# Softmax cross-entropy on one core: loads on two DMA rings, three buffers, a tapered last group and one activation table set

## The chip, the cores and the metric

The kernel runs on one core of a Trainium2 chip. The metric is device time in microseconds (us), lower is better. The times of before agree within 0.03% (2439.7 to 2440.5 us). In the profile, ACT is ScalarE, DVE is VectorE, POOL is GpSimd, SP is SyncE; "ACTq" and "SPq" are the instruction sequencers of ScalarE and SyncE; the timelines list their DMA issues there. A "ring" below is a DMA queue of the page. In these traces the loads that SyncE issues are on q1 (21,168 packets, 1048.65 MB in the kernel before), those that ScalarE issues on q10, and GpSimd's gathers on q0, which the page calls software_dynamic (2048 packets before).

## The reference

For 8192 rows of 32,000 float32 logits, the loss is log(sum(exp(row))) minus the logit at the row's label. The reference subtracts the row's maximum first; both kernels leave that out, and results are correct on the drawn data.

```python
logits_max = np.max(logits, axis=-1, keepdims=True)
log_sum_exp = np.log(np.sum(np.exp(logits - logits_max), axis=-1)) + logits_max.squeeze(-1)
log_probs = logits - log_sum_exp[..., np.newaxis]
loss = -log_probs[np.arange(batch)[:, None], np.arange(seq), labels]
```

The logits are 1048.6 MB and are read once. The result is 32 KB.

## The kernel before

128 partitions hold 64 rows each ("groups" g of 128 rows). 61 groups are loaded in two pieces of 128x16000 (8.19 MB each) into two buffers; the last three in pieces of 128x4000 into five. All loads are issued from SyncE. ScalarE computes exp in place and sums it on the way. GpSimd gathers the label logits, one small indirect DMA for each group.

```python
data_pool = ctx.enter_context(tc.tile_pool(name="data", bufs=2))
fine_pool = ctx.enter_context(tc.tile_pool(name="fine", bufs=5))
# ... labels through SyncE, index arithmetic on GpSimd ...
for g in range(G):
    nc.gpsimd.indirect_dma_start(out=lab_logit[:, g:g + 1], out_offset=None, in_=lg,
        in_offset=bass.IndirectOffsetOnAxis(ap=idx[:, g:g + 1], axis=1))
# ...
for g in range(G):
    if g >= G - FINE_GROUPS:
        ...                                   # the same with 128x4000 pieces
    else:
        for c in range(C):
            t = data_pool.tile([P, W], FP32)
            nc.sync.dma_start(out=t[:], in_=lg_pg[:, g, c * W:(c + 1) * W])
            nc.scalar.activation(out=t[:], in_=t[:], func=mybir.ActivationFunctionType.Exp,
                                 accum_out=stats_col(g, c))
# ... finalize(lo, hi): reduce_sum on DVE, Ln on ACT, subtract, store; called for 63 groups, then for 1
```

The semaphores and the order of each engine's instructions are made by a scheduler from this text. The place of a load in ScalarE's program is the scheduler's choice.

The softmax here doesn't subtract the row's maximum and nothing guards it: scores larger than these inputs give would overflow.

## Time and profile before

| | before |
|---|---|
| time, median | 2440.0 us |
| DMA | 430 GB/s over the span, engines at 90% or more in every slice but the last |
| ScalarE busy | 72% |
| one 128x16000 load, one after the other | 18.90 us |
| exp of 128x16000 | 13.54 us |
| last byte to end of the profile's span | 8.4 us |

The page of the kernel before. In section 2 each figure is one of 40 equal slices: DMA is the busy share of the 16 DMA engines in tenths. A group of section 5 is "line engine op, names, shapes, count | busy us, mean ns | idle before it, and what ended the idle time". A row of section 6 ends with KB and the median us from issue to landing.

```profile
span 2438.7 us, 851 instructions
## 1 busy us (share of the span) xinstructions
DVE 1.7 (0%) x5; ACT 1754.4 (72%) x298; POOL 61.2 (3%) x70
...
DMA  9999999999999999999999999999999999999998
GB/s 404 437 420 422 435 437 435 429 429 437 437 436 428 431 435 437 435 432 428 435 436 436 435 427 434 436 437 435 427 432 436 437 435 425 434 437 432 426 430 360
...
L85 ACT ACTIVATE t<-t 128x16000 f32<-128x16000 f32 x122 | 1651.4, 13536 | 642.9 <-DMA t<-in_logits_dram 642.9
...
t<-in_logits_dram SPq DMA_DIRECT2D x122, 8000.0 KB, 24.1
```

DMA is the limit. ScalarE's 643 us of idle time are waits for loads, and 24.1 us from issue to landing are 18.9 us of transfer behind 5.2 us left of the load in flight: with one ring and two buffers there is always a load queued. The timeline of the middle shows it (start us, duration us, engine, line, operation; in brackets the idle time before it):

```profile
992.28 13.54 ACT L85 ACTIVATE t<-t 128x16000 f32<-128x16000 f32 x1 [5.28 <-DMA t<-in_logits_dram]
...
1011.17 13.54 ACT L85 ACTIVATE t<-t 128x16000 f32<-128x16000 f32 x1 [5.26 <-DMA t<-in_logits_dram]
...
1030.06 13.54 ACT L85 ACTIVATE t<-t 128x16000 f32<-128x16000 f32 x1 [5.27 <-DMA t<-in_logits_dram]
```

One exp each 18.90 us, like a clock. In the trace's packet records each of the 16 engines moves 8 packets of 64,000 B per load, 2.36 us each, back to back, and the next load's first packet follows without a gap. Between 400 and 2350 us the engines moved 433.2 GB/s and were idle for 0.3 us on average.

While loads run, the small gathers mostly advance by 4.8 us, about the length of two 2.36 us packets (43 of the 63 steps take 4.6 to 4.8 us; two lines of the gathers):

```profile
13.76 0.94 POOL L57 DMA_INDIRECT lab_logit<-in_logits_dram,idx  x1 [0.34 <-DMA lab_logit<-in_logits_dram,idx]
18.55 0.94 POOL L57 DMA_INDIRECT lab_logit<-in_logits_dram,idx  x1 [3.85 <-DMA lab_logit<-in_logits_dram,idx]
```

And the end: the last exp starts 0.5 us after the last byte (2430.3), then come an activation table load, Ln and the store.

```profile
2430.84 3.54 ACT L76 ACTIVATE tf<-tf 128x4000 f32<-128x4000 f32 x1 [1.11 <-DMA tf<-in_logits_dram]
...
2434.49 1.28 ACT L101 ACT_TABLE_LOAD   x1
...
2436.21 0.34 ACTq L109 DMA_DIRECT2D out_dram<-res  x1
```

### The profile page before, as it was taken

The numbers are of one execution on the slowest core, as the hardware profiler recorded it, in microseconds if no ns is written. First come the engines' busy times: TensorE is split into PE (matmuls) and PEld (weight loads), VectorE is DVE, ScalarE is ACT, GpSimd is POOL, SyncE is SP. The second block draws the span as 40 slices with busy tenths as digits, with TensorE's granted clock in tenths as the row PEclk, the third lists the DMA queues.
The fourth block names the chain that finished last, engine by engine and source line by source line (L and its number), as shares of the span: only waits on it lengthen the run. The fifth ranks groups of instructions, "written<-read, shape, count | busy, mean of one in ns | idle before, by whom it ended". The sixth has DMA issues, their size and how long they took to land.

```text
span 2438.7 us, 851 instructions
## 1 busy us (share of the span) xinstructions
DVE 1.7 (0%) x5; ACT 1754.4 (72%) x298; POOL 61.2 (3%) x70
## 2 busy tenths in 40 slices
DVE  0000000000000000000000000000000000000000
ACT  4777766777677767777677767777677767777697
POOL 3222000000000000000000000000000000000000
DMA  9999999999999999999999999999999999999998
GB/s 404 437 420 422 435 437 435 429 429 437 437 436 428 431 435 437 435 432 428 435 436 436 435 427 434 436 437 435 427 432 436 437 435 425 434 437 432 426 430 360
DMA packets 23510, 1048.77 MB, mean 430 GB/s; under 512 B 4688, under 2 KB 4816, under 8 KB 4816
## 3 DMA queue, kind: packets, MB, share of 16 engines
q1 hardware_dynamic: 21168, 1048.65, 99.6%
q0 software_dynamic: 2048, 0.04, 0.1%
q10 hardware_dynamic: 288, 0.03, 0.0%
q14 instruction: 6, 0.05, 0.0%
HBM read 1048.67 MB, written 0.03 MB: 430 GB/s over the span
## 4 chain that ended last, share of the span: by engine, by line
DMA 63%; ACT 36%; issue 0%; ACTq 0%; SPq 0%; DVE 0%
DMA t<-in_logits_dram 61%; ACT t L85 34%; DMA tf<-in_logits_dram 2%; ACT tf L76 2%; ACT L101 0%; ACT L76 0%; ACTq L85 0%; ACT logsum L101 0%; SPq L84 0%; DVE res L105 0%; SPq L48 0%; ACTq L109 0%; ACTq L76 0%
## 5 line engine op out<-in xcount | busy, mean ns | idle before, releaser
L85 ACT ACTIVATE t<-t 128x16000 f32<-128x16000 f32 x122 | 1651.4, 13536 | 642.9 <-DMA t<-in_logits_dram 642.9
L76 ACT ACTIVATE tf<-tf 128x4000 f32<-128x4000 f32 x24 | 84.7, 3530 | 14.6 <-DMA tf<-in_logits_dram 14.6
L57 POOL DMA_INDIRECT lab_logit<-in_logits_dram,idx x64 | 60.5, 945 | 186.8 <-DMA lab_logit<-in_logits_dram,idx 184.2
L85 ACT ACTIVATION_READ_ACCUMULATOR t<-t 128x1 f32 x122 | 22.7, 186 | 0.0
L85 ACT ACT_TABLE_LOAD x1 | 1.3, 1283 | 23.3 <-DMA t<-in_logits_dram 23.3
L76 ACT ACTIVATION_READ_ACCUMULATOR tf<-tf 128x1 f32 x24 | 4.5, 187 | 0.0
L101 ACT ACT_TABLE_LOAD x2 | 2.6, 1283 | 0.0
L96 DVE TENSOR_REDUCE totals<-stats 128x63 f32<-128x504 f32 x1 | 0.7, 678 | 2394.9 <-ACT tf L76 2394.9
L76 ACT ACT_TABLE_LOAD x1 | 1.3, 1283 | 0.8 <-DVE res L105 0.8
L66 DVE MEMSET stats<- 128x504 f32 x1 | 0.5, 478 | 0.9 <-PEq L127 0.9
L101 ACT ACTIVATE logsum<-totals 128x63 f32<-128x63 f32 (+1 forms) x2 | 0.5, 229 | 0.0
L105 DVE TENSOR_TENSOR res<-logsum,lab_logit 128x63 f32<-128x63 f32 (+1 forms) x2 | 0.4, 192 | 2.2 <-ACT logsum L101 2.2
L53 POOL TENSOR_TENSOR idx<-idx,labs 128x64 int32<-128x64 int32 x1 | 0.3, 318 | 1.8 <-DMA labs<-in_labels_dram 1.8
L96 DVE TENSOR_REDUCE totals<-stats_last 128x1 f32<-128x8 f32 x1 | 0.2, 161 | 36.4 <-ACT tf L76 36.4
L51 POOL IOTA idx<- 128x64 int32 x1 | 0.2, 172 | 0.4 <-PEq L138 0.4
L127 POOL MEMSET const-uint8-127<- 128x1 uint8 x1 | 0.1, 118 | 0.0
L127 POOL MEMSET const-bfloat16-1.0<- 128x1 bf16 x1 | 0.1, 113 | 0.0
L127 POOL MEMSET const-float32-0.0<- 128x1 f32 x1 | 0.1, 98 | 0.2 <-issue 0.2
L127 POOL MEMSET const-float32-1.0<- 128x1 f32 x1 | 0.1, 104 | 0.0
## 6 DMA issues: line engine op xcount, KB each, us to landing
t<-in_logits_dram SPq DMA_DIRECT2D x122, 8000.0 KB, 24.1
tf<-in_logits_dram SPq DMA_DIRECT2D x24, 2000.0 KB, 20.1
lab_logit<-in_logits_dram,idx POOLq DMA_INDIRECT x64, 33.4
labs<-in_labels_dram SPq DMA_DIRECT2D x1, 64.0 KB, 1.9
out_dram<-res ACTq DMA_DIRECT2D x1, 31.5 KB, 9.1
out_dram<-res ACTq DMA_DIRECT2D x1, 0.5 KB, 1.4
```

What stands on the lines that cost most here:

```text
L51: nc.gpsimd.iota(idx[:], pattern=[[V, G]], base=0, channel_multiplier=G * V)
L53: nc.gpsimd.tensor_tensor(out=idx[:], in0=idx[:], in1=labs32, op=mybir.AluOpType.add)
L57: nc.gpsimd.indirect_dma_start(out=lab_logit[:, g:g + 1], out_offset=None, in_=lg, in_offset=bass.IndirectOffsetOnAxis(ap=idx[:, g:g + 1], ...
L66: nc.vector.memset(stats[:], 0.0)
L76: nc.scalar.activation(out=tf[:], in_=tf[:], func=mybir.ActivationFunctionType.Exp, accum_out=stats_col(g, c),)
L85: nc.scalar.activation(out=t[:], in_=t[:], func=mybir.ActivationFunctionType.Exp, accum_out=stats_col(g, c),)
L96: nc.vector.reduce_sum(out=totals[:, lo:hi], in_=stats[:, lo:hi, :] if hi <= G - 1 else stats_last[:], axis=mybir.AxisListType.X,)
L101: nc.scalar.activation(out=logsum[:, lo:hi], in_=totals[:, lo:hi], func=mybir.ActivationFunctionType.Ln,)
L105: nc.vector.tensor_tensor(out=res[:, lo:hi], in0=logsum[:, lo:hi], in1=lab_logit[:, lo:hi], op=mybir.AluOpType.subtract,)
L127: nc = _bacc.Bacc("TRN2", target_bir_lowering=False, num_devices=1)
```

## The change

Its intent: keep more loads outstanding by alternating them between the SyncE and ScalarE rings with three buffers; shorten the end by cutting the last group into pieces that shrink from 11,200 to 600 columns; load one table set for both exp and Ln, once. The labels are now loaded from GpSimd.

```diff
-    data_pool = ctx.enter_context(tc.tile_pool(name="data", bufs=2))
-    fine_pool = ctx.enter_context(tc.tile_pool(name="fine", bufs=5))
+    data = ctx.enter_context(tc.tile_pool(name="data", bufs=3))
+    TAPER = [11200, 8000, 5600, 3500, 2000, 1100, 600]
+    rings = [nc.sync, nc.scalar]
+    n_loads = 0
+    def load(dst, src):
+        nonlocal n_loads
+        rings[n_loads % 2].dma_start(out=dst, in_=src)
+        n_loads += 1
...
-    nc.sync.dma_start(out=labs64[:], in_=labels_pg)
+    nc.gpsimd.dma_start(out=labs64[:], in_=labels_pg)
+    nc.scalar.preload_act_table_set("natural_log_exp_and_others")
...
-    for g in range(G):          # 128x16000 pieces, the last three groups in 128x4000
+    for g in range(G - 1):
+        for c in range(C):
+            t = data.tile([P, W], FP32, tag="t")
+            load(t[:], lg_pg[:, g, c * W:(c + 1) * W])
+            nc.scalar.activation(out=t[:], in_=t[:], func=EXP, accum_out=sums[:, g, c:c + 1])
...
+    spaces = [[0, 3, 5], [1, 2, 4], [6]]       # which taper pieces share a buffer
...
+    for i, n in enumerate(TAPER):
+        load(place[i], lg_pg[:, G - 1, starts[i]:starts[i] + n])
+    for i, n in enumerate(TAPER):
+        nc.scalar.activation(out=place[i], in_=place[i], func=EXP, accum_out=sums_last[:, i:i + 1])
...
+    nc.scalar.activation(out=logsum_last[:], in_=sums_last[:, NT - 1:NT], func=LN, bias=part[:])
```

As built, ScalarE's program in the steady state is: load k, load k+2, exp k, exp k+1, exp k+2, exp k+3, load k+4, load k+6, and so on (k odd). SyncE issues the even loads, each when its buffer is free.

More of the change, by code (lines that the diff above doesn't have):

```diff
@@ L7 @@
 from concourse._compat import with_exitstack
+from concourse.masks import make_identity
 FP32 = mybir.dt.float32
 I32 = mybir.dt.int32
+EXP = mybir.ActivationFunctionType.Exp
+LN = mybir.ActivationFunctionType.Ln
+ALU = mybir.AluOpType
 @with_exitstack
@@ L23 @@
     B, S, V = logits.shape
-    N = B * S
     P = 128
-    G = N // P
-    assert N % P == 0
+    G = B * S // P
     W = 16000
     C = V // W
-    assert V % W == 0
-    WF = 4000
-    CF = V // WF
-    FINE_GROUPS = 3
-    assert V % WF == 0
     lg = logits.rearrange("b s v -> (b s) v")
@@ L41 @@
     out_pg = out.rearrange("b s -> (b s)").rearrange("(p g) -> p g", g=G)
-    data_pool = ctx.enter_context(tc.tile_pool(name="data", bufs=2))
-    fine_pool = ctx.enter_context(tc.tile_pool(name="fine", bufs=5))
+    data = ctx.enter_context(tc.tile_pool(name="data", bufs=3))
     persist = ctx.enter_context(tc.tile_pool(name="persist", bufs=1))
+    TAPER = [11200, 8000, 5600, 3500, 2000, 1100, 600]
+    assert sum(TAPER) == V
+    NT = len(TAPER)
+    rings = [nc.sync, nc.scalar]
[4 more added lines that the diff above has]
+        n_loads += 1
     labs64 = persist.tile([P, G], mybir.dt.int64)
-    nc.sync.dma_start(out=labs64[:], in_=labels_pg)
+    nc.gpsimd.dma_start(out=labs64[:], in_=labels_pg)
+    nc.scalar.preload_act_table_set("natural_log_exp_and_others")
+    labs32 = labs64[:].bitcast(I32).rearrange("p (g two) -> p g two", two=2)[:, :, 0]
     idx = persist.tile([P, G], I32)
     nc.gpsimd.iota(idx[:], pattern=[[V, G]], base=0, channel_multiplier=G * V)
-    labs32 = labs64[:].bitcast(I32).rearrange("p (g two) -> p g two", two=2)[:, :, 0]
-    nc.gpsimd.tensor_tensor(out=idx[:], in0=idx[:], in1=labs32, op=mybir.AluOpType.add)
+    nc.gpsimd.tensor_tensor(out=idx[:], in0=idx[:], in1=labs32, op=ALU.add)
     lab_logit = persist.tile([P, G], FP32)
-    for g in range(G):
+    for g in [G - 1] + list(range(G - 1)):
         nc.gpsimd.indirect_dma_start(
@@ L62 @@
         )
-    stats = persist.tile([P, G - 1, CF], FP32)
-    stats_last = persist.tile([P, 1, CF], FP32)
-    nc.vector.memset(stats[:], 0.0)
-    def stats_col(g, c):
-        return stats[:, g, c:c + 1] if g < G - 1 else stats_last[:, 0, c:c + 1]
-    for g in range(G):
-        if g >= G - FINE_GROUPS:
-            for c in range(CF):
-                tf = fine_pool.tile([P, WF], FP32)
-                nc.sync.dma_start(out=tf[:], in_=lg_pg[:, g, c * WF:(c + 1) * WF])
-                nc.scalar.activation(
-                    out=tf[:], in_=tf[:],
-                    func=mybir.ActivationFunctionType.Exp,
-                    accum_out=stats_col(g, c),
-                )
-        else:
-            for c in range(C):
-                t = data_pool.tile([P, W], FP32)
-                nc.sync.dma_start(out=t[:], in_=lg_pg[:, g, c * W:(c + 1) * W])
-                nc.scalar.activation(
-                    out=t[:], in_=t[:],
-                    func=mybir.ActivationFunctionType.Exp,
-                    accum_out=stats_col(g, c),
-                )
@@ L91 @@
-    totals = persist.tile([P, G], FP32)
-    logsum = persist.tile([P, G], FP32)
-    res = persist.tile([P, G], FP32)
-    def finalize(lo, hi):
-        nc.vector.reduce_sum(
-            out=totals[:, lo:hi],
-            in_=stats[:, lo:hi, :] if hi <= G - 1 else stats_last[:],
-            axis=mybir.AxisListType.X,
-        )
-        nc.scalar.activation(
-            out=logsum[:, lo:hi], in_=totals[:, lo:hi],
-            func=mybir.ActivationFunctionType.Ln,
-        )
-        nc.vector.tensor_tensor(
-            out=res[:, lo:hi], in0=logsum[:, lo:hi], in1=lab_logit[:, lo:hi],
-            op=mybir.AluOpType.subtract,
-        )
-        nc.scalar.dma_start(out=out_pg[:, lo:hi], in_=res[:, lo:hi])
@@ L111 @@
-    finalize(0, G - 1)
-    finalize(G - 1, G)
+    sums = persist.tile([P, G, C], FP32)
+    for g in range(G - 1):
[3 more added lines that the diff above has]
+            nc.scalar.activation(out=t[:], in_=t[:], func=EXP, accum_out=sums[:, g, c:c + 1])
+    sums_last = persist.tile([P, NT], FP32)
+    spaces = [[0, 3, 5], [1, 2, 4], [6]]
+    starts = [sum(TAPER[:i]) for i in range(NT)]
+    place = {}
@@ new lines @@
+    for s in spaces:
+        t = data.tile([P, W], FP32, tag="t")
+        o = 0
+        for i in s:
+            place[i] = t[:, o:o + TAPER[i]]
+            o += TAPER[i]
+    for i, n in enumerate(TAPER):
+        load(place[i], lg_pg[:, G - 1, starts[i]:starts[i] + n])
+    for i, n in enumerate(TAPER):
+        nc.scalar.activation(out=place[i], in_=place[i], func=EXP, accum_out=sums_last[:, i:i + 1])
+    totals = persist.tile([P, G - 1], FP32)
+    logsum = persist.tile([P, G - 1], FP32)
@@ new lines @@
+    res = persist.tile([P, G - 1], FP32)
+    nc.vector.reduce_sum(out=totals[:], in_=sums[:, 0:G - 1, :], axis=mybir.AxisListType.X)
+    nc.scalar.activation(out=logsum[:], in_=totals[:], func=LN)
+    nc.vector.tensor_tensor(out=res[:], in0=logsum[:], in1=lab_logit[:, 0:G - 1], op=ALU.subtract)
+    nc.scalar.dma_start(out=out_pg[:, 0:G - 1], in_=res[:])
+    part = persist.tile([P, 1], FP32)
+    nc.vector.reduce_sum(out=part[:], in_=sums_last[:, 0:NT - 1], axis=mybir.AxisListType.X)
+    logsum_last = persist.tile([P, 1], FP32)
@@ L116 @@
+    res_last = persist.tile([P, 1], FP32)
+    nc.scalar.activation(out=logsum_last[:], in_=sums_last[:, NT - 1:NT], func=LN, bias=part[:])
+    nc.vector.tensor_tensor(out=res_last[:], in0=logsum_last[:], in1=lab_logit[:, G - 1:G], op=ALU.subtract)
+    nc.scalar.dma_start(out=out_pg[:, G - 1:G], in_=res_last[:])
 _INS = ['logits', 'labels']
```

## The prediction

> **What bounds it now.** DMA. The page's slices show the DMA engines at 90% or more throughout, 430 GB/s over the span; ScalarE (ACT) is busy 72%, and of its idle time 643 us is waits for `t` loads. The timeline shows one exp every 18.90 us for one 8.19 MB load. A single 64,000 B packet takes 2.36 us in the trace; 8 per engine make 18.9, with no gap between loads. One ring and two buffers already keep the engines full: an exp takes 13.54 us, so each load is queued about 5 us before the one in flight ends (24.1 us from issue to landing = 5.2 + 18.9). Estimate of the floor: 128 loads' worth x 18.9 = 2419 us. The other 20: 2.3 until the first packet, about 10 lost mostly while the 64 gathers run (first 300 us: intervals 19.1 to 19.6), 8 of tail (last landing at 2430.8, end at 2438.7).
>
> **What the change can gain.** Almost nothing in the stream. One table load of 1.28 us at the end, label load off the ring (0.4), shorter last exp (0.7 instead of 3.5): at best 5 us.
>
> **What it adds.**
> (1) Two rings share the same 16 engines. [...] The trace agrees: while loads run, gathers mostly advance every 4.8 us, two turns of one 2.36 us packet. So two loads in flight on two rings halve each other: both land after about 37.8 us, instead of one at 18.9 and one at 37.8. Loads land in pairs and buffers come free late.
> (2) ACT's order as built: loads k, k+2, then four exps, the fourth with two waits. The trace of before shows such a double wait split: an EVENT_SEMAPHORE holds ACT's sequencer until the load lands, then the exp. So ACT's next loads are issued only when the fourth exp's load has landed. SP's next load needs the exp two before that to end, 41.8 us (estimate: three exps + issue) after a pair landed, while only about 40 us of DMA work was left. Both rings run dry once in every four loads.
>
> **Cost of one dry spell**, estimated from durations: landing to semaphore 0.45, dispatch 0.2, issue to first packet 1.05 (1.17 to 2.27 in the first load), and slower first packets (3.0 instead of 2.36: +0.3 to 0.7). About 2.3 us, 30 times: +70 us (40 to 85).
> (3) The tail: the last pieces also share rings and land nearly together behind backed-up exps; ACT ends about 9 us after the last byte. Where the taper should save 3 us, I expect 3 to 5 lost.
>
> Sum: 2440 - 3 + 70 + 4 = about 2511 us. DMA average falls to about 418 GB/s.
>
> **Signs.** Right: exps no longer at even 18.9 intervals but in a pattern of four repeating every 77.5 to 78.3 us (before 75.6); issue to landing of `t` about 35 to 50 us; some 30 DMA gaps of 1.5 to 2.5 us, each ended by load issues from ACT just after a landing and SP at the same time; 64,000 B packets still about 2.36 us when one ring is active; last ACT exps back to back after the last landing. Wrong: four exps in 75.6 us.
>
> **What would make it wrong.** If an engine drains a whole load before it changes ring (loads then land in order, no dry spells): about 2436, same. If the ACT sequencer runs past the double wait, its loads are issued in time: about 2440. If the gaps are shorter, between 2465 and 2490. Faster by over 2% would need 2391, below the floor at this packet rate.
>
> Faster 0.02, within 2% 0.26, slower 0.72. Range 2475 to 2530.

The durations in the cost of a dry spell are to be found in the trace of before: 0.45 us from a load's last byte to its landing, 0.08 from there to the exp and 0.12 from an exp's end to SyncE's next issue (together the 0.2), 1.1 from the first load's issue to its first packet, and 3.0 us (mean) for the first 16 packets.

## The result, and the profile after

| | before | after |
|---|---|---|
| time, median | 2440.01 us | 2522.88 us (2522.23 to 2523.39, 4 runs) |
| ratio to before | 1 | 1.0339 (95% interval 1.0324 to 1.0354) |
| DMA over the span | 430 GB/s | 416 GB/s |
| idle core-wide DMA gaps over 0.1 us in the stream | 0 | 31, mean 1.52 us |
| last byte at | 2430.3 us | 2508.5 us |
| last byte to end of span | 8.4 us | 13.1 us |

Ratios are the mean time of one kernel's fast runs over that of the other's fast runs in the same rounds, so they are not quite the ratio of the medians quoted. The profiled runs of before and after are both fast.

The page of the kernel after, the lines that answer to those shown of before:

```profile
span 2521.6 us, 626 instructions
...
DVE 0.8 (0%) x4; ACT 1737.0 (69%) x269; POOL 62.4 (2%) x71
...
DMA  9999999999999999999999999999999999999997
GB/s 407 422 406 406 421 412 434 406 422 422 406 439 420 408 421 407 439 406 422 421 407 439 409 419 415 413 438 407 419 409 422 424 420 422 408 420 422 422 420 327
...
L81 ACT ACTIVATE t<-t 128x16000 f32<-128x16000 f32 x126 | 1704.0, 13524 | 780.9 <-DMA t<-in_logits_dram 780.8
...
t<-in_logits_dram SPq DMA_DIRECT2D x63, 8000.0 KB, 40.1
t<-in_logits_dram ACTq DMA_DIRECT2D x63, 8000.0 KB, 41.1
```

The exp still takes 13.5 us and DMA still shows 9 in nearly every slice: a share in tenths hides the idle time measured below (2.1 us in each 78.2). The GB/s row doesn't. From issue to landing a load now takes 40 us instead of 24. The timeline of one period of four loads, all of ScalarE's program and of SyncE's issues:

```profile
1041.03 13.54 ACT L81 ACTIVATE t<-t 128x16000 f32<-128x16000 f32 x1 [24.00 <-DMA t<-in_logits_dram]
...
1054.57 13.52 ACT L81 ACTIVATE t<-t 128x16000 f32<-128x16000 f32 x1
...
1068.09 13.52 ACT L81 ACTIVATE t<-t 128x16000 f32<-128x16000 f32 x1
1081.30 0.33 ACTq L55 DMA_DIRECT2D t<-in_logits_dram  x1
1081.51 0.19 ACT L81 ACTIVATION_READ_ACCUMULATOR t<-t 128x1 f32 x1
1081.60 13.52 ACT L81 ACTIVATE t<-t 128x16000 f32<-128x16000 f32 x1
1081.72 0.33 SPq L55 DMA_DIRECT2D t<-in_logits_dram  x1
...
1119.23 13.54 ACT L81 ACTIVATE t<-t 128x16000 f32<-128x16000 f32 x1 [24.01 <-DMA t<-in_logits_dram]
```

Four exps run back to back, then ScalarE waits 24 us. The period is 78.2 us (1041.03 to 1119.23) where four loads of before took 75.6. The next table shows three stretches of that period (stretch and length in us, busy time of DVE, ACT, POOL, TensorE clock, DMA share, GB/s; the share and rate count a packet where it starts, so they can pass 1):

```profile
1041.03:1080.40 39.37, 0.00 (x0) 39.37 (x5) 0.00 (x0) 1.00 0.96 416
1080.70:1082.10 1.40, 0.00 (x0) 1.40 (x3) 0.00 (x0) 1.00 0.00 0
1082.10:1119.23 37.13, 0.00 (x0) 13.12 (x3) 0.00 (x0) 1.00 1.04 441
```

From 1080.7 to 1082.1 us no byte moves. Both rings are empty, because ScalarE's next load leaves at 1081.30 and SyncE's at 1081.72, and the first packet starts at 1082.28, about 1 us after. I call this a dry spell. There are 31, one in every four loads. Going through the packet records from 400 to 2350 us (25 spells): each spell costs 2.1 us of idle time averaged over the engines (1.5 with none active, the rest ragged edges), and the packets after it are slow (mean of all 64,000 B packets 2383.6 ns against 2365.3 in the one-ring kernel E1 below; the median is 2361), another 0.6 us; at the spell shown the first 16 packets take 3.0 us in the mean. That is about 2.6 us a spell.

The end of the timeline after:

```profile
2490.23 9.52 ACT L97 ACTIVATE t<-t 128x11200 f32<-128x11200 f32 x1
...
2506.60 4.85 ACT L97 ACTIVATE t<-t 128x5600 f32<-128x5600 f32 x1
...
2517.51 0.69 ACT L97 ACTIVATE t<-t 128x600 f32<-128x600 f32 x1
...
2519.11 0.45 ACTq L114 DMA_DIRECT2D out_dram<-res_last  x1
```

All seven last exps run without waiting for data: ScalarE is behind, and ends 9.7 us after the last byte.

So the 82.9 us are: 79.4 in the dry spells (the stream ends at 2508.5; in E2 below, which has the same rings and no dry spell, at 2429.1), plus 4.7 in the tail (13.1 instead of 8.4), minus 1.2 for the stream without dry spells (2429.1 against 2430.3).

### The profile page after: what moved, and what is told of

Read it like the earlier page. It is cut to its first block, busy times and chain, and to the rows that moved or that the text cites. A ratio compares the mean times of both kernels' runs of the same rounds, so it can differ in the third digit from the quotient of the medians.

```text
span 2521.6 us, 626 instructions
## 1 busy us (share of the span) xinstructions
DVE 0.8 (0%) x4; ACT 1737.0 (69%) x269; POOL 62.4 (2%) x71
## 5 line engine op out<-in xcount | busy, mean ns | idle before, releaser
L81 ACT ACTIVATE t<-t 128x16000 f32<-128x16000 f32 x126 | 1704.0, 13524 | 780.9 <-DMA t<-in_logits_dram 780.8
L97 ACT ACTIVATE t<-t 128x11200 f32<-128x11200 f32 (+6 forms) x7 | 28.0, 3995 | 0.0
```

The lines of the kernel that those rows point to most:

```text
L81: nc.scalar.activation(out=t[:], in_=t[:], func=EXP, accum_out=sums[:, g, c:c + 1])
L97: nc.scalar.activation(out=place[i], in_=place[i], func=EXP, accum_out=sums_last[:, i:i + 1])
```

## The experiments

Theory: two loads on two rings share the engines, so they land in pairs and late; ScalarE's loads are stuck in its program behind exps; together both rings run dry. Rivals: two rings make the engines slower; the taper, three buffers or the table set cost the time; issuing from ScalarE slows its exps; only the tail lost. All kernels below gave correct results. Each is an edit of the changed kernel.

### E1: every load on SyncE's ring

```diff
-    rings = [nc.sync, nc.scalar]
+    rings = [nc.sync, nc.sync]
```

> The changed kernel with every load on the SyncE ring; three buffers, taper and single table load stay. Ring theory (two loads in flight halve each other, then both rings run dry once in four loads): exps come at even 18.9 us, no dry spells between the first packet and the last, 2433 to 2438 us, so 84 us or more come back. Rival A (three buffers, the taper, or the table set cost the time): stays above 2500. Rival B (ACT-side work got slower): stays above 2500.

Measured: 2439.0 us (2438.8 to 2439.2, 5 runs), ratio to before 0.9995 (0.9981 to 1.0009). The exps come at even 18.9 us, no dry spell, 433.3 GB/s between 400 and 2350 us. It missed the upper end of my range by 1 us, but 84 us came back with this one line. Buffers, taper and table set do not cost the time. They also gain only about 1 us by the medians, and the interval of the ratio includes 1. Why they gain so little is a second question; the end of its timeline answers it:

```profile
2406.20 9.54 ACT L97 ACTIVATE t<-t 128x11200 f32<-128x11200 f32 x1 [0.77 <-DVE res L105]
...
2433.50 0.69 ACT L97 ACTIVATE t<-t 128x600 f32<-128x600 f32 x1
```

The last byte is there at 2428.9, and the last exp starts 4.6 us later. These pieces, each 0.71 of the one before or less, arrive about as fast as, or faster than, ScalarE can take them (an exp of 8000 columns takes 6.85 us; the load of the next 5600 is estimated at 6.6, from 18.90 us for 16,000), and 1.4 us of Ln work sits in front of them (2404.83 to 2406.20). So the tail is 8.4 us, as before.

### E2: both rings, but each of ScalarE's loads earlier in its program

```diff
-            load(t[:], lg_pg[:, g, c * W:(c + 1) * W])
-            nc.scalar.activation(out=t[:], in_=t[:], func=EXP, accum_out=sums[:, g, c:c + 1])
...                # chunks: all (g, c) in order; fetch(k): tile and load of piece k
+    for k in range(3):
+        fetch(k)
+    for k, (g, c) in enumerate(chunks):
+        t = tiles.pop(k)
+        nc.scalar.activation(out=t[:], in_=t[:], func=EXP, accum_out=sums[:, g, c:c + 1])
+        if k + 3 < len(chunks):
+            fetch(k + 3)
```

The instructions are the same; as built, ScalarE now has one load between every two exps instead of two loads between every four.

> Both rings, three buffers as changed, but the loop is written so that load k+3 follows exp k; as built ACT has one load between every two exps and no exp with two waits ahead of a load. Ring-plus-order theory: loads still share (issue to landing near 40 us, landings in pairs), but none of the 31 dry spells remain; about 2440 to 2447 us, a few us more than one ring because the last pieces share rings and ACT ends about 10 us after the last byte. Rival C (two rings make the 16 engines slower by themselves, packet switching, contention): stays above 2490 and 64,000 B packets take longer than 2.37 us. Rival D (only the tail lost): no change from 2523 beyond 10 us.

Measured: 2445.9 us (2445.6 to 2446.2, 5 runs), ratio 1.0024 (1.0010 to 1.0037). No dry spell. The loads share the rings about as much as in the changed kernel (its page: the rate in 40 slices, and the loads of the two rings):

```profile
GB/s 420 434 421 435 422 434 434 421 436 436 436 434 431 431 432 436 436 436 434 434 428 432 435 435 436 435 433 431 433 433 435 436 435 433 432 432 433 435 432 307
...
t<-in_logits_dram SPq DMA_DIRECT2D x63, 8000.0 KB, 38.3
t<-in_logits_dram ACTq DMA_DIRECT2D x63, 8000.0 KB, 36.6
```

The rate between 400 and 2350 us is 433.2 GB/s, the packet median 2366 ns, as in E1. So two rings by themselves cost this stream nothing (rival C falls), and the whole 79 us of the stream came from where ScalarE's loads stand in its program. The 6.9 us over E1 are tail: 14.9 us from last byte to end, because the last pieces queue at ScalarE: its seven last exps run back to back from 2412.61, and end 11.5 us after the last byte (2429.1). Nor did a second issuing engine make the stream any faster: 433.3 GB/s in E1, 433.2 in E2.

ScalarE's loads are still late in E2. The timeline of one of them:

```profile
1030.92 0.19 ACT L89 ACTIVATION_READ_ACCUMULATOR t<-t 128x1 f32 x1
1041.11 13.54 ACT L89 ACTIVATE t<-t 128x16000 f32<-128x16000 f32 x1 [10.00 <-DMA t<-in_logits_dram]
1041.12 0.33 ACTq L55 DMA_DIRECT2D t<-in_logits_dram  x1
```

Its buffer is free from 1031.1, but it leaves only with the start of the next exp: as built, the load stands behind one exp more than the one that frees its buffer (in the changed kernel every other load stands behind two more). In the steady state ScalarE's loads leave 8.3 to 10.2 us after their buffers come free; in the changed kernel every other one is mostly 13.1 us late. What differs is what is left in the rings at that moment: the packets still to be started are 0.22 to 0.36 of a load in E2, and none at the dry spells of the changed kernel. A late load cost nothing here (no dry spell), because SyncE's load was still in flight.

### E3: every load on ScalarE's ring

```diff
-    rings = [nc.sync, nc.scalar]
+    rings = [nc.scalar, nc.scalar]
```

> The changed kernel with every load on the ScalarE ring. Loads are then in one order and nothing shares; ACT issues all 133 loads. Ring theory: like one ring on SyncE, 2433 to 2445 us. Rival E (issuing loads from ScalarE delays its exps and so the loads): above 2480.

Measured: 2593.2 us (2593.0 to 2594.5, 5 runs), ratio 1.0629. My expectation failed by 150 us, and it is the most useful run. With one ring nothing shares, yet the engines ran dry 63 times, once in two loads. Its timeline:

```profile
1035.29 13.54 ACT L81 ACTIVATE t<-t 128x16000 f32<-128x16000 f32 x1 [8.11 <-DMA t<-in_logits_dram]
1048.74 0.19 ACT L81 ACTIVATION_READ_ACCUMULATOR t<-t 128x1 f32 x1
1054.18 13.54 ACT L81 ACTIVATE t<-t 128x16000 f32<-128x16000 f32 x1 [5.26 <-DMA t<-in_logits_dram]
1054.19 0.82 ACTq L55 DMA_DIRECT2D t<-in_logits_dram  x2
```

The program is "two exps, two loads". The buffer of the second of these loads has been free since 1048.9, when the exp of 1035.29 ended, and that of the first since the exp before that; but both leave at 1054.19 and just after, in the instant in which the exp ahead of them in the program gets its data. In 63 cases the first load of the two leaves 7 to 10 ns after the start of that exp. These exps wait for one semaphore only. The load's own wait does not explain the delay: it is for the semaphore that ScalarE's exps raise, which rose at 1048.93 and then not before 1067.82. So in these runs a load issued from ScalarE is held by the exp ahead of it until that exp's data has landed, whether the exp waits for one thing or two. (An exp is two instructions, ACTIVATE and ACTIVATION_READ_ACCUMULATOR; which of the two holds the load is not shown.) The exp's data is the last thing in the ring, so the ring is empty at that moment. Rival E had foretold a time above 2480, and that came true, but not by its mechanism (issuing delays the exps): the exp still takes 13.54 us, and its waits are for data.

The same holding is to be seen in the start of the changed kernel, with an exp that waits for one semaphore and is third in line:

```profile
55.21 13.52 ACT L81 ACTIVATE t<-t 128x16000 f32<-128x16000 f32 x1
61.19 0.34 ACTq L55 DMA_DIRECT2D t<-in_logits_dram  x1
68.64 0.19 ACT L81 ACTIVATION_READ_ACCUMULATOR t<-t 128x1 f32 x1
68.73 13.52 ACT L81 ACTIVATE t<-t 128x16000 f32<-128x16000 f32 x1
```

The load at 61.19 needs a buffer that came free at 55.2. It leaves when the load of the exp at 68.73 has landed (61.16), not when that exp starts: here it is held by the semaphore, not by the engine.

Here the spells cost (2584.4 - 2428.9) / 63 = 2.5 us each against E1, by the ends of the streams. In the changed kernel it is (2508.5 - 2429.1) / 31 = 2.6 us each against E2.

### E4: ScalarE issues every third load

```diff
-    rings = [nc.sync, nc.scalar]
+    rings = [nc.sync, nc.sync, nc.scalar]
...
-        rings[n_loads % 2].dma_start(out=dst, in_=src)
+        rings[n_loads % 3].dma_start(out=dst, in_=src)
```

> As changed, but ScalarE issues only every third load (SyncE two of three). Theory, refined by the ScalarE-ring-only run: a load issued from ScalarE leaves only when the load of the exp ahead of it in ScalarE's program has landed, whether that exp has one wait or two; where SyncE's next load is not queued by then, both rings run dry. Replaying the built order with the durations of the trace (2.36 us per packet, exp 13.53, issue to first packet 1.05) gives a dry spell in every three loads, 41 in all, each shorter (about 1 us, plus the slower first packets), 2500 to 2525 us. Rival (dry spells come from loads sharing two rings half and half): with a third fewer loads on ScalarE and less sharing, clearly under 2490.

Measured: 2552.7, 2548.3, 2512.8 and 2552.4 us; ratio of the runs counted as fast 1.037 (1.0304 to 1.0437). The profile shows 40 dry spells, one in three loads, as expected, but with a mean of 1.50 us with no engine active where I had about 1. All four runs are above 2490, so the rival (less sharing, fewer dry spells) falls. The size I had too small: by the ends of the streams a spell costs (2532.0 - 2429.1) / 40 = 2.6 us against E2, as in the changed kernel, and the tail takes 18.9 us. This profile is of a run counted as slow (2552.7, more than 1.5% above the fastest of this kernel, at full clock). The run at 2512.8, inside my range, was not profiled, so why it was shorter stays open; the ratio above rests on it and the run at 2548.3 alone.

### E5: ScalarE issues every fourth load

As E4, with three `nc.sync` to one `nc.scalar` and `n_loads % 4`.

> As changed, but ScalarE issues only every fourth load. Same theory: ScalarE's loads are issued as late as before, but SyncE always has a load queued behind, so the engines stay full: no dry spells in the stream (two or three short ones among the last pieces), 2450 to 2462 us. If the mere presence of two rings or of loads on ScalarE cost time, it would lie in proportion to the number of such loads, near 2480.

Measured: 2447.3 us (2446.6 to 2447.4, 4 runs), ratio 1.0028 (1.0013 to 1.0044); 3 us under my range. No dry spell at all, also not in the tail, 433.3 GB/s between 400 and 2350 us. The kernel still has 31 of its 126 big loads on ScalarE's ring, so loads on ScalarE do not cost time in proportion to their number. But the premise of my expectation was wrong: these loads are not "issued as late as before". The first of them:

```profile
35.96 0.19 ACT L81 ACTIVATION_READ_ACCUMULATOR t<-t 128x1 f32 x1
36.18 0.38 ACTq L55 DMA_DIRECT2D t<-in_logits_dram  x1
44.29 13.54 ACT L81 ACTIVATE t<-t 128x16000 f32<-128x16000 f32 x1 [8.14 <-DMA t<-in_logits_dram]
```

As built, the load stands directly behind the exp that frees its buffer, and all 31 leave 0.03 us after that. So this run shows loads on ScalarE that are not held; that a held load costs nothing while SyncE's is in flight is shown by E2, not here. What is left over E1 is tail (16.2 us from last byte to end).

### E6: six buffers of 128x8000 in place of three of 128x16000

```diff
-    W = 16000
+    W = 8000
...
-    data = ctx.enter_context(tc.tile_pool(name="data", bufs=3))
+    data = ctx.enter_context(tc.tile_pool(name="data", bufs=6))
...
-    TAPER = [11200, 8000, 5600, 3500, 2000, 1100, 600]
+    TAPER = [8000, 8000, 5600, 4000, 2800, 2000, 1000, 600]
...
-    spaces = [[0, 3, 5], [1, 2, 4], [6]]
+    spaces = [[0], [1], [2, 5], [3, 4], [6], [7]]
```

> As changed, with the same bytes of buffers as six of 128x8000 instead of three of 128x16000; loads still alternate between the rings and ScalarE still issues in pairs behind exps. Theory: twice as many loads are queued in finer steps, so another load is always outstanding when ScalarE waits: no dry spells, 2446 to 2460 us ([...]the tail loses as in the changed kernel). Rival (two rings with ScalarE's order are bad at any grain): above 2500.

Measured: 2486.7 us (2479.0 to 2489.6, 4 runs), ratio 1.0184 (1.0168 to 1.0200). Half right: there is no moment in which all engines are idle, but the time is 27 us over my range. Going through the packets from 400 to 2350 us, the engines are idle for 12.3 us on average, each at another moment, and packets are slow after it (mean 1197 ns of 32,000 B, median 1185, about 1620 per engine: some 20 us more). My estimate had treated 16 engines as one. They are spread: the 16 completions of one load in this trace lie 1.7 us apart in the median, and I take it that the early engines run dry while the late ones still work. That is argued, not shown: spread alone does not do it, since in E2 it is 3.6 us and the engines are idle for 0.4 us between 400 and 2350 us.

### E7: one ring, and a taper that ScalarE can follow

```diff
-    rings = [nc.sync, nc.scalar]
+    rings = [nc.sync, nc.sync]
...
-    TAPER = [11200, 8000, 5600, 3500, 2000, 1100, 600]
+    PIECES = [(G - 2, 12000), (G - 2, 10000), (G - 2, 10000)]
+    PIECES += [(G - 1, n) for n in [8000, 6300, 5000, 4000, 3100, 2400, 1850, 1350]]
+    SLOTS = [[0], [1], [2], [3, 5, 8], [4, 6, 7, 9], [10]]
...                # sums of the first 62 groups are finished after the first piece, the last two together
```

> One ring on SyncE, three buffers, one table set, and the taper spread over the last two groups so that each exp takes no longer than the next piece's load (next piece at least 0.707 of the last plus about 120 columns); the sums of the other groups are finished before it. With the changed kernel's taper on one ring the last exps ran back to back and ended 5.4 us after the last byte. Expected: last exp ends about 2 us after the last byte, 2435 to 2437.5 us, 0.1 to 0.2% under the kernel before. If tail backlog is not the cause: 2439 or more.

Measured: 2436.5 us (2435.9 to 2436.8, 5 runs), ratio to before 0.9985 (0.9971 to 0.9998). It is the only version whose interval lies below before: 0.15%, small but where it was expected. The 0.707 of the expectation comes from the exps of 8000 and 16000 columns (6.85 and 13.54 us) against 18.90 us for a load of 16000. The end of its timeline (last byte at 2429.3):

```profile
2419.24 3.54 ACT L107 ACTIVATE t<-t 128x4000 f32<-128x4000 f32 x1 [0.36 <-DMA t<-in_logits_dram]
...
2429.88 1.31 ACT L107 ACTIVATE t<-t 128x1350 f32<-128x1350 f32 x1
...
2431.94 0.34 ACTq L91 DMA_DIRECT2D out_dram<-res  x1
```

The pieces now wait for data almost to the end, the last exp starts 0.6 us after the last byte, and the tail is 5.4 us instead of 8.4.

## Why the prediction was right or wrong

The time was right: 2511 us predicted, range 2475 to 2530, 2522.9 measured, "slower" as expected. Point by point:

- **What bounds it now (DMA), the floor (2419) and the gain (at best 5 us): right.** E1 has all of the change but the second ring, and its median is 1.2 us below before. The 3 us that I took off in the sum were too much, since the taper saved nothing (tail 8.4 us before and in E1).
- **Dry spells, one in four loads: right.** I said about 30, with gaps of 1.5 to 2.5 us and a period of 77.5 to 78.3; it is 31, gaps of 1.52 us on average, a period mostly of 78.0 to 78.5 (in some stretches 75.6 and 80.9 in turn). Both issues coincide as foretold: ScalarE's at 1081.30, SyncE's at 1081.72.
- **Their cost: the term that was mis-sized.** I took 2.3 us each, 70 in all, from durations of the trace; the ends of the streams give 2.6 each, 79.4 in all. What I left out are the ragged edges: at the spell shown, the last 16 packets end between 1080.20 and 1080.76 us, the landing comes after the last of them (1081.16), and the next 16 start between 1082.28 and 1082.91.
- **Tail: right.** 3 to 5 us lost were foretold, 4.7 were lost; the last four pieces land between 2506.3 and 2509.0, and ScalarE ends 9.7 us after the last byte (foretold about 9).
- **Step (1), sharing: the fact was right, its place in the reasoning too large.** Two loads in flight do halve each other: the loads that SyncE and ScalarE issued 0.42 us apart at 1003 us landed 4.7 us apart at 1041.0 and 1045.7, and from 1009 to 1038 us the packet records of the two rings alternate one by one on all 16 engines, in packets of 64,000 B, 2.36 us each. But E2 shares as much and has no dry spell, and E3 shares nothing and has twice as many. Sharing is neither enough nor needed. In the changed kernel it is what makes SyncE's next load late too (it waits for three exps that start late because their loads landed together), so that SyncE can't cover for ScalarE. That last sentence is argued from the timeline; I have no run that isolates it.
- **Step (2), the held load: right in effect, but its reason is not needed.** I put it down to exps with two waits. In the changed kernel's trace such a split wait is there: 29 of the 31 held loads leave within 0.2 us after an EVENT_SEMAPHORE of ScalarE. But E3 has only exps with one wait ahead of its loads, and holds them just the same. In one of my conditions, "If the ACT sequencer runs past the double wait", the word "double" should not have been there. Nor is holding enough: E2 holds its loads for 8.3 to 10.2 us and has no dry spell. The dry spells of these runs have both: a held load, and nothing else left in the rings when it leaves.

Open: E4's two times; the idle time of single engines in E6; the share of sharing in SyncE's lateness; which instruction of an exp holds the load behind it.

## What to carry to other kernels

Before adding a ring or a buffer to hide DMA, look whether the engines have a gap at all: here 18.9 us per load, exactly 8 packets, left nothing to hide, and no version with a second issuing engine was faster (E2 and E5: 0.2 to 0.3% slower, all of it in the tail). A load issued from ScalarE stood in line behind exps that waited for data, so it was issued when the data it was meant to overlap had just landed. Look in the trace where the scheduler put the load: directly behind the instruction that frees its buffer it left at once (E5), and one exp further on it was 8.3 to 10.2 us late, which was harmless only while the other ring had a load in flight (E2). Or keep the stream on an engine with no other work (E1). Taper the last pieces by no more than the consumer can follow: next piece's load time at least the exp time of the one before (E7, tail 5.4 us; 8.4 with the steeper taper of E1). Each time the rings ran dry cost about 2.5 us (63 times in E3) or 2.6 (31 in the changed kernel), of which 1.5 us in the changed kernel with no engine active.
